# Second norm on GpSimd and ScalarE, output projection in two double banks of PSUM

## Chip, core and metric

The kernel runs on one core of a Trainium2 chip. The metric is the device time of one execution in microseconds. The kernel before took 1049.43 us (median of 3 runs, 1049.25 to 1049.82).

## What is computed

One decoder block on x of 1024 tokens by 1024 features, in float32: RMSNorm, input projection, eight heads of forgetting attention beside a gated spatial mix, output projection with residual, a second RMSNorm, a gated MLP with a causal convolution of width 3, residual, and a final RMSNorm. The part that the change touches is this:

```python
def rmsnorm(x, gain):
    xf = x.astype(jnp.float32)
    y = xf * lax.rsqrt(jnp.mean(xf * xf, axis=-1, keepdims=True) + EPS)
    return y.astype(x.dtype) * gain
...
        mix = jnp.concatenate([att, sg], axis=-1)
        h = h + mix @ w_out[layer]
        h = h + conv_ffn(rmsnorm(h, norm_ffn_g[layer]), w_up[layer], conv_w[layer],
                         conv_b[layer], w_down[layer])
```

## The kernel before

Every float32 product on PE is written as three passes over rounded parts: high by high, high by low, low by high. A "split" makes the two parts: ScalarE (ACT) rounds the value, VectorE (DVE) subtracts the rounded part (`split_w`, L157 to L166). The big products are done in seven instead of eight block products, so sums and differences of blocks of the weights and of the activations are needed as well.

The program is written in the order of the work, and a scheduler that builds each engine's instruction stream decides what stands where. Each engine then works its stream strictly in order. `after(tc, a, b)` (L64) tells the scheduler that a may not stand ahead of b.

Attention (L1138 on) works through eight heads. For each head PE makes the logits of a block of 128 queries in a place of PSUM that is two banks wide (`place()`, two such places, tag "L", four banks), DVE and ACT turn them into weights in SBUF, PE turns these around (`turn_p`, L1026), ACT rounds and DVE subtracts (L1027, L1028), and PE multiplies them with the values (L1042). The turned blocks and the value sums lie in the four other banks (tag "b"). Head 7 has no logits of a next head beside it. After it, the last pair of heads is scaled (`pair_half(3)`, L955 to L958: DVE, ACT, DVE), once the sums of its rows have come back by DMA (L943).

Then comes the stage of the change, the output projection and the second norm (L1196 to L1365). Eight tiles of 128 tokens, in the order 0, 4, 1, 5, 2, 3, 6, 7. Each has two halves of 512 columns, `hf` 0 and 1, and each half takes 12 matmuls of 128x512: four pairs of heads k = 0 to 3 by three passes (`wmm`, L1279 to L1281). k = 3 needs the last pair of heads (the tile G_3837 in the instruction streams).

- At the start of the stage the PSUM pool of attention is given back and a new one with eight single banks is taken (four "b", four "s"). For the first four tiles (0, 4, 1, 5), k = 0 to 2 of all eight halves, 72 matmuls, come before the first matmul with k = 3.
- `hadd` (L1289, DVE) adds a half to the residual that was loaded into `h2`.
- `norm2` (L1296 to L1300): ACT squares the tile from SBUF into the SBUF tile `xn` with a running sum, takes the root; DVE takes the reciprocal and makes `xn` = h2 * r * gain in one instruction of 128x1024 (L1299). `h2` is stored to DRAM.
- `flip` (L1317 on): PE turns `xn` around in two groups of four 128x128 transposes into two "s" banks; ACT and DVE split the result into the operands `XB` of the MLP (B11, B21 from tiles 0 to 3; T2, T3 from tiles 4 to 7).
- Beside this, the first two weight blocks of the MLP are prepared: `upw_a` splits A11 and A12 on ACT and DVE (L166, tiles `wha`), `upw_b(..., inplace=True)` makes four sums of blocks on GpSimd (POOL, L1251 to L1259).

After tile 7, PE starts the MLP's products (`product`, L1372): two with B11 and B21, then the turn of tile 7, two more, then those with T2 and T3. The MLP and the down projection fill the rest of the time.

Of the kernel before, what the change touches and what calls it, by code (L numbers as in the profile page):

```python
# [14 lines left out]
P = 128  # L15
# [54 lines left out]
def block_kernel(ctx: ExitStack, tc: tile.TileContext, xT, xtok, wuv, wv0, wva, wvk, wvl, wqk, cpk, bfv,  # L70
# [1030 lines left out]

    STEPS = [[(h, g) for g in GROUPS[n:n + 2]] for h in range(8) for n in range(0, 9, 2)]
# [99 lines left out]
    psa.release()  # L1202
    psa = tc.alloc_tile_pool(name="psc", bufs=4, space=bass.MemoryType.PSUM, reuse_waits="tile")
# [39 lines left out]
    def upw_b(i, out, inplace=False):  # L1243
# [5 lines left out]
        if inplace:  # L1249
            s = [a21, ut_(upl, "sg", [P, 512], F32, 4), a11, a12]  # L1250
            pool.tensor_tensor(out=a11, in0=a21, in1=a11, op=ALU.add)  # L1251
            pool.tensor_tensor(out=s[1], in0=a11, in1=a22, op=ALU.add)
            pool.tensor_tensor(out=a21, in0=a21, in1=a22, op=ALU.add)
        else:
            s = [ut_(upl, "sg", [P, 512], F32, 4) for _ in range(4)]
            pool.tensor_tensor(out=s[0], in0=a21, in1=a22, op=ALU.add)  # L1256
            pool.tensor_tensor(out=s[1], in0=s[0], in1=a11, op=ALU.add)  # L1257
            pool.tensor_tensor(out=s[2], in0=a21, in1=a11, op=ALU.add)
        pool.tensor_tensor(out=s[3], in0=s[1], in1=a12, op=ALU.add)  # L1259
# [13 lines left out]
    normed = {}  # L1273

    def wmm(tt, hf, ps, ks_):
        ts_ = slice(tt * P, (tt + 1) * P)
        for k in ks_:
            w = wo[k][hf]
            pe.matmul(ps, attT[k][:, 0, ts_], w[:, 0, :], start=(k == 0), stop=False)  # L1279
            pe.matmul(ps, attT[k][:, 0, ts_], w[:, 1, :], start=False, stop=False)  # L1280
            pe.matmul(ps, attT[k][:, 1, ts_], w[:, 0, :], start=False, stop=(k == 3))  # L1281
# [5 lines left out]
    def hadd(tt, hf, ps):  # L1287
        o = slice(hf * 512, hf * 512 + 512)
        x = dve.tensor_tensor(out=h2[tt][:, o], in0=ps, in1=h2[tt][:, o], op=ALU.add)  # L1289
        if tt == 5:  # L1290
            after(tc, x, normed[1])

    def norm2(tt):
        xn[tt] = ut_(xtp, "xn", [P, 1024], F32, 2)
        r = ss2[:, tt:tt + 1]
        act.activation(xn[tt], h2[tt], AF.Square, accum_out=r)  # L1296
        act.activation(r, r, AF.Sqrt, bias=eps[:, 0:1], scale=1.0 / 1024)
        dve.reciprocal(r, r)
        normed[tt] = dve.scalar_tensor_tensor(out=xn[tt], in0=h2[tt], scalar=r, in1=g2b, op0=ALU.mult, op1=ALU.mult)  # L1299
        sp.dma_start(out=h2d[tt], in_=h2[tt])  # L1300
# [8 lines left out]
    def flip(tt):  # L1309
# [3 lines left out]
        for kh in range(2):  # L1313
            ps = sbank()
            for j in range(4):
                k = 4 * kh + j
                pe.transpose(ps[:, j * P:(j + 1) * P], xn[tt][:, k * P:(k + 1) * P], ident)  # L1317
            pp.append(ps.rearrange("p (k t) -> p k t", k=4))
# [17 lines left out]

    WA = [upw_a(i) for i in range(AHEAD)]
    W = [WA[0][1](("A11", "A12"))]
    first = (0, 4, 1, 5)
    banks8 = {(tt, hf): (bank() if hf == 0 else sbank()) for tt in first for hf in range(2)}  # L1340
    for hf in range(2):
        for tt in first:
            wmm(tt, hf, banks8[tt, hf], (0, 1, 2))
# [475 lines left out]
```

## Time and profile before

| | |
|---|---|
| time, median of 3 | 1049.43 us |
| the profiled execution's own time | 1049.38 us |
| span of its trace | 1047.7 us |
| PE busy | 1037.6 us, 99% of the span |
| DVE busy | 891.8 us, 85% |
| ACT busy | 563.4 us, 54% |
| POOL busy | 217.7 us, 21% |
| granted TensorE clock | 0.999 |
| the stage of the change | 360.82 us (first matmul of the projection) to 410.27 us (first product of the MLP) |

Times in the trace are counted from the start of the span. A row of the timeline has start, length, engine, line, operation, output and inputs, the number of instructions that were merged, and in brackets how long the engine had been idle and who released it. PE is the matmul itself and PEld the load of its weights. Matmuls overlap: one of 128x512 is listed with 0.39 us but the next starts some 0.23 us after it. The engine queue of DMA issues is SPq.

### The profile page before, as it was taken

The numbers are of one execution on the slowest core, as the hardware profiler recorded it, in microseconds if no ns is written. First come the engines' busy times: TensorE is split into PE (matmuls) and PEld (weight loads), VectorE is DVE, ScalarE is ACT, GpSimd is POOL, SyncE is SP. The second block draws the span as 40 slices with busy tenths as digits, with TensorE's granted clock in tenths as the row PEclk, the third lists the DMA queues.
The fourth block names the chain that finished last, engine by engine and source line by source line (L and its number), as shares of the span: only waits on it lengthen the run. The fifth ranks groups of instructions, "written<-read, shape, count | busy, mean of one in ns | idle before, by whom it ended". The sixth has DMA issues, their size and how long they took to land.

```text
span 1047.7 us, 14269 instructions
## 1 busy us (share of the span) xinstructions
PE 1037.6 (99%) x4998; PEld 869.5 (83%) x4998; DVE 891.8 (85%) x1302; ACT 563.4 (54%) x1003; POOL 217.7 (21%) x165
## 2 busy tenths in 40 slices
PE   9999999999999999999999999999999999999997
PEld 6988888988888888788888888888888888888886
DVE  6898887888888779998999989898997866897774
ACT  6777632457767747644444444444444544454654
POOL 0000241500422540253333323323331000000000
PEclk9999999999999999999999999999999999999999
DMA  9622558795745533232254431432322998333432
GB/s 326 237 87 86 159 155 245 224 260 174 205 138 171 184 139 141 80 103 79 96 174 162 131 121 60 131 121 70 131 81 81 320 336 297 105 98 101 142 119 101
DMA packets 67451, 161.66 MB, mean 154 GB/s; under 512 B 8094, under 2 KB 9238, under 8 KB 67380
## 3 DMA queue, kind: packets, MB, share of 16 engines
q1 hardware_dynamic: 67108, 160.72, 47.7%
q8 instruction: 39, 0.64, 0.3%
q14 instruction: 32, 0.26, 0.1%
q10 hardware_dynamic: 272, 0.04, 0.0%
HBM read 115.68 MB, written 45.05 MB: 153 GB/s over the span
## 4 chain that ended last, share of the span: by engine, by line
PE 92%; DVE 3%; DMA 2%; ACT 1%; issue 1%; SPq 1%; ACTq 0%; DVEq 0%
PE k L1632 20%; PE qc L1372 11%; PE qa L1372 11%; PE qd L1372 11%; PE qb L1372 5%; PE ps L270 5%; PE pb L270 5%; PE pb L1042 3%; PE pb L1026 2%; PE qc L510 2%; PE qa L510 2%; PE qd L510 2%; PE pl L979 2%; PE pl L978 2%; PE pf L1066 1%; PE pf L1068 1%
## 5 line engine op out<-in xcount | busy, mean ns | idle before, releaser
L1632 PE MATMUL k<-whb,wha 128*128 128x512 f32 (+1 forms) x936 | 209.9, 386 | 0.0
L1632 PEld LDWEIGHTS k<-whb,wha 128*128 128x128 f32 x936 | 174.1, 188 | 35.8 <-DVE wha L166 0.2
L1372 PE MATMUL qc<-xT,whb 128*128 128x512 f32 x540 | 129.9, 389 | 0.1
L1372 PE MATMUL qa<-xB,wha 128*128 128x512 f32 x528 | 127.4, 390 | 0.0
L1372 PEld LDWEIGHTS qc<-xT,whb 128*128 128x128 f32 x540 | 101.3, 188 | 21.6 <-ACT whb L160 0.5
L1372 PEld LDWEIGHTS qa<-xB,wha 128*128 128x128 f32 x528 | 98.8, 188 | 20.8 <-DVE wha L166 0.4
L160 ACT CAST wha<-sg 128x512 fp32r<-128x512 f32 x77 | 47.8, 622 | 96.9 <-PE k L1632 83.9
L160 ACT CAST whb<-sg 128x512 fp32r<-128x512 f32 x82 | 50.6, 618 | 87.3 <-PE qc L1372 67.1
L166 DVE TENSOR_TENSOR wha<-sg,wha 128x512 fp32r<-128x512 f32 x77 | 52.8, 687 | 39.2 <-ACT wha L160 39.1
L1372 PE MATMUL qd<-xB,whb 128*128 128x512 f32 x264 | 63.7, 389 | 0.0
L1372 PE MATMUL qd<-xT,whb 128*128 128x512 f32 x264 | 63.7, 389 | 0.0
L1372 PE MATMUL qb<-xT,whb 128*128 128x512 f32 x252 | 61.0, 389 | 0.0
L166 DVE TENSOR_TENSOR whb<-sg,whb 128x512 fp32r<-128x512 f32 x82 | 57.0, 697 | 4.4 <-ACT whb L160 4.3
L1027 ACT CAST pt<-pb 128x512 fp32r<-128x512 f32 x72 | 40.4, 584 | 37.5 <-PE pb L1026 32.5
L1256 POOL TENSOR_TENSOR sg<-raw 128x512 f32<-128x512 f32 x20 | 30.8, 1541 | 140.3 <-DVE whb L166 78.1
L1372 PEld LDWEIGHTS qd<-xT,whb 128*128 128x128 f32 x264 | 49.5, 188 | 10.5 <-DVE u L1479 0.3
L1372 PEld LDWEIGHTS qd<-xB,whb 128*128 128x128 f32 x264 | 49.6, 188 | 10.3
L1028 DVE TENSOR_TENSOR pt<-pb,pt 128x512 fp32r<-128x512 f32 x72 | 47.4, 687 | 10.7 <-ACT pt L1027 10.4
L1372 PEld LDWEIGHTS qb<-xT,whb 128*128 128x128 f32 x252 | 47.2, 188 | 10.0 <-DVE whb L166 0.3
L1042 PE MATMUL pb<-pt,V 128*128 128x512 f32 (+3 forms) x192 | 49.6, 362 | 0.4 <-DVE pt L1028 0.3
L1259 POOL TENSOR_TENSOR sg<-sg,raw 128x512 f32<-128x512 f32 x20 | 33.3, 1667 | 63.5 <-DVE whb L166 63.5
L1257 POOL TENSOR_TENSOR sg<-sg,raw 128x512 f32<-128x512 f32 x20 | 34.8, 1740 | 47.5 <-issue 44.9
(426 smaller groups left out, 2241.1 us busy)
## 6 DMA issues: line engine op xcount, KB each, us to landing
raw<-wup SPq DMA_DIRECT2D x44, 512.0 KB
sg<-hx SPq DMA_DIRECT2D x77, 256.0 KB
hx<-hs SPq DMA_DIRECT2D x44, 256.0 KB
hx<-ca SPq DMA_DIRECT2D x35, 256.0 KB
xT<-wdn SPq DMA_DIRECT2D x28, 256.0 KB
x<-kd SPq DMA_DIRECT2D x24, 256.0 KB
A<-xtok SPq DMA_DIRECT2D x8, 512.0 KB
raw<-wqk SPq DMA_DIRECT2D x8, 512.0 KB
```

Source lines behind the costliest of these rows:

```text
L160: act.copy(h, src)
L166: return eng.tensor_tensor(out=l, in0=src, in1=f32(h), op=ALU.subtract)
L270: pe.matmul(banks[m], xs(n, xi, k)[:, ms], w[:, wi, :], start=(first and k == 0 and c == 0 and (own or m % 2 == 0)), stop=(k == 3 and c == ...
L510: pe.matmul(ps, w[:, wi, ks], xs(n, xi, k), start=(first and c == 0), stop=(c == 11), skip_group_check=True)
L1027: casts.append(act.copy(pt[:, 0, :], ptr))
L1028: los.append(dve.tensor_tensor(out=pt[:, 1, :], in0=ptr, in1=f32(pt[:, 0, :]), op=ALU.subtract))
L1042: seq(pe.matmul(po[half][:, o:o + w], lhs, pt[:, s, c:c + w], start=(new and s == 0), stop=(s == 1 and (half, k) in ((1, 6), (0, 3))), ski ...
L1256: pool.tensor_tensor(out=s[0], in0=a21, in1=a22, op=ALU.add)
L1257: pool.tensor_tensor(out=s[1], in0=s[0], in1=a11, op=ALU.add)
L1259: pool.tensor_tensor(out=s[3], in0=s[1], in1=a12, op=ALU.add)
L1372: pe.matmul(ps, w[:, wi, ks], xb[:, xi, k, :], start=(first and n == 0), stop=(n == 11), skip_group_check=True)
L1632: pe.matmul((banks[bk + m] if ps is None else ps)[:, o], xh[:, xi, ms], wh[:, wi, o], start=((first and p_ == 0 or new) and n == 0), stop= ...
```

## The change

- **The pool.** Attention's PSUM pool stays until the end of the stage. A tile of the projection takes one of the two wide places (`half_of`): `wide[tt]` is 128x1024, and each half is one of its banks. So two tiles can be open, where it was four. `first` shrinks to (0, 4): 36 matmuls come before k = 3. The turns use the four "b" banks, and `flip` gets a floor: its transposes stand behind the last matmul that was written before it.
- **The norm.** After each `hadd`, POOL multiplies the half by the gain into `xn` (128x512). ACT squares the tile with `wide[tt]`, the place in PSUM, as the target that nobody reads. After DVE's reciprocal, ACT scales `xn` in place by r (Copy, 128x1024). DVE's instruction at L1299 is gone.
- **The sums** of the two early weight blocks on POOL are put into four pairs, each behind the gain of the tile 1, 5, 2 or 3.
- The order in which the turns stand: tile 0 is turned between the halves of tile 1, the others behind the next tile's second half.

```diff
+    def half_of(tt, hf):
+        if tt not in wide:
+            wide[tt] = place()
+        return wide[tt][:, hf * 512:hf * 512 + 512]
...
-    psa.release()
-    psa = tc.alloc_tile_pool(name="psc", bufs=4, space=bass.MemoryType.PSUM, reuse_waits="tile")
...
+            sums_ = ((a11, a21, a11), (s[1], a11, a22), (a21, a21, a22), (a12, s[1], a12))
+            ops = [lambda o=o: pool.tensor_tensor(out=o[0], in0=o[1], in1=o[2], op=ALU.add) for o in sums_]
+            parts.extend((ops[:2], ops[2:]))
...
     def hadd(tt, hf, ps):
         o = slice(hf * 512, hf * 512 + 512)
-        x = dve.tensor_tensor(out=h2[tt][:, o], in0=ps, in1=h2[tt][:, o], op=ALU.add)
-        if tt == 5:
-            after(tc, x, normed[1])
+        dve.tensor_tensor(out=h2[tt][:, o], in0=ps, in1=h2[tt][:, o], op=ALU.add)
+        if hf == 0:
+            xn[tt] = ut_(xtp, "xn", [P, 1024], F32, 2)
+        gained[tt] = pool.tensor_tensor(out=xn[tt][:, o], in0=h2[tt][:, o], in1=g2b[:, o], op=ALU.mult)

     def norm2(tt):
-        xn[tt] = ut_(xtp, "xn", [P, 1024], F32, 2)
         r = ss2[:, tt:tt + 1]
-        act.activation(xn[tt], h2[tt], AF.Square, accum_out=r)
+        act.activation(wide[tt], h2[tt], AF.Square, accum_out=r)
         act.activation(r, r, AF.Sqrt, bias=eps[:, 0:1], scale=1.0 / 1024)
         dve.reciprocal(r, r)
-        normed[tt] = dve.scalar_tensor_tensor(out=xn[tt], in0=h2[tt], scalar=r, in1=g2b, op0=ALU.mult, op1=ALU.mult)
+        act.activation(xn[tt], xn[tt], AF.Copy, scale=r)
         sp.dma_start(out=h2d[tt], in_=h2[tt])
...
-    first = (0, 4, 1, 5)
-    banks8 = {(tt, hf): (bank() if hf == 0 else sbank()) for tt in first for hf in range(2)}
+    first = (0, 4)
...
     for tt in (0, 4, 1, 5, 2, 3, 6, 7):
         hload(tt)
         for hf in range(2):
-            if tt in first:
-                wmm(tt, hf, banks8[tt, hf], (3,))
-                hadd(tt, hf, banks8[tt, hf])
-            else:
-                ps = bank()
-                wmm(tt, hf, ps, range(4))
-                hadd(tt, hf, ps)
+            m = wmm(tt, hf, half_of(tt, hf), (3,) if tt in first else range(4))
+            hadd(tt, hf, half_of(tt, hf))
+            if tt == 1 and hf == 0:
+                flip(0, m)
         norm2(tt)
-        if prev is not None:
-            flip(prev)
+        if prev:
+            flip(prev, m)
         prev = tt
+        if tt in (1, 5, 2, 3):
+            for o in parts.pop(0):
+                after(tc, o(), gained[tt])
     late.release()
...
+    psa.release()
+    psa = tc.alloc_tile_pool(name="psc", bufs=4, space=bass.MemoryType.PSUM, reuse_waits="tile")
```

What the scheduler makes of it is seen in the engines' streams. First PE at the end of head 7. The names are the tiles with their numbers: pb are the single banks, pl the wide places, whl and G the weights of the projection or the pairs of heads, pt the turned attention weights, V the values. Before, the last value products are followed by the projection:

```order
L1042 MATMUL pb_3826<-pt_3787,V_1734 128x256 x2
L1042 MATMUL pb_3826<-pt_3795,V_1733 128x512 x2
L1042 MATMUL pb_3826<-pt_3815,V_1733 128x384 x2
L1042 MATMUL pb_3826<-pt_3815,V_1734 128x128 x2
L1279 MATMUL pb_3876<-whl_3715,A_2849 128x512
L1280 MATMUL pb_3876<-whl_3715,A_2849 128x512
```

In the changed kernel the same place reads so:

```order
L1042 MATMUL pb_3826<-pt_3787,V_1734 128x256 x2
L1042 MATMUL pb_3826<-pt_3795,V_1733 128x512 x2
L1106 MATMUL pl_3872<-whl_3723,A_3281 128x512
L1042 MATMUL pb_3826<-pt_3815,V_1733 128x384
L1107 MATMUL pl_3872<-whl_3723,A_3281 128x512
L1108 MATMUL pl_3872<-whl_3723,A_3281 128x512
L1042 MATMUL pb_3826<-pt_3815,V_1733 128x384
L1042 MATMUL pb_3826<-pt_3815,V_1734 128x128 x2
L1106 MATMUL pl_3872<-G_3731,G_3684 128x512
```

Three matmuls of tile 0 (pl_3872) have moved in among the last value products; three more (k = 0) stand singly among the turns ahead of them, so six of the projection's matmuls now stand inside attention.

Then PE at the first matmuls with k = 3 and behind them. Before, each half has its own bank (pb_3876 and ps_3877 are the halves of tile 0, pb_3878 and ps_3879 those of tile 4), and the row that follows the 24 of them is tile 2 in another bank:

```order
L1279 MATMUL pb_3876<-G_3738,G_3837 128x512
L1280 MATMUL pb_3876<-G_3738,G_3837 128x512
L1281 MATMUL pb_3876<-G_3738,G_3837 128x512
L1279 MATMUL ps_3877<-G_3738,G_3837 128x512
L1280 MATMUL ps_3877<-G_3738,G_3837 128x512
L1281 MATMUL ps_3877<-G_3738,G_3837 128x512
L1279 MATMUL pb_3878<-G_3738,G_3837 128x512
```

In the changed kernel tiles 0 (pl_3872) and 4 (pl_3882) alternate, and tile 1 (pl_3960) follows in the place of tile 0:

```order
L1108 MATMUL pl_3872<-G_3738,G_3837 128x512
L1106 MATMUL pl_3882<-G_3738,G_3837 128x512
L1107 MATMUL pl_3882<-G_3738,G_3837 128x512
L1108 MATMUL pl_3882<-G_3738,G_3837 128x512
L1106 MATMUL pl_3872<-G_3738,G_3837 128x512
L1107 MATMUL pl_3872<-G_3738,G_3837 128x512
L1108 MATMUL pl_3872<-G_3738,G_3837 128x512
L1106 MATMUL pl_3882<-G_3738,G_3837 128x512
L1107 MATMUL pl_3882<-G_3738,G_3837 128x512
L1108 MATMUL pl_3882<-G_3738,G_3837 128x512
L1106 MATMUL pl_3960<-whl_3715,A_2849 128x512
```

The second L1106 on pl_3872 (the second half of tile 0) carries a wait for DVE's addition of the first half, because both halves now belong to one tile of PSUM; so does the second half of every tile. The L1106 on pl_3960 carries a wait for ACT's Square of tile 0, the last user of that place.

Last DVE at the same place, where wha are the first weight blocks of the MLP. This is the changed kernel:

```order
L166 TENSOR_TENSOR wha_3866<-raw_3862,wha_3866 128x512
L166 TENSOR_TENSOR wha_3869<-raw_3862,wha_3869 128x512
L166 TENSOR_TENSOR wha_3910<-raw_3864,wha_3910 128x512
L166 TENSOR_TENSOR wha_3913<-raw_3864,wha_3913 128x512
L1295 TENSOR_TENSOR pt_3922<-pl_3872,pt_3922 128x512
L1295 TENSOR_TENSOR pt_3940<-pl_3882,pt_3940 128x512
L1295 TENSOR_TENSOR pt_3922<-pl_3872,pt_3922 128x512
```

And before, with the same four splits ahead of the first addition:

```order
L166 TENSOR_TENSOR wha_3956<-raw_3868,wha_3956 128x512
L166 TENSOR_TENSOR wha_3959<-raw_3868,wha_3959 128x512
L1289 TENSOR_TENSOR pt_3976<-pb_3876,pt_3976 128x512
L1289 TENSOR_TENSOR pt_3976<-ps_3877,pt_3976 128x512
L1289 TENSOR_TENSOR pt_3992<-pb_3878,pt_3992 128x512
```

The four splits still stand ahead of the first addition; what moved is the additions' order, first halves of tiles 0 and 4 and then the second ones.

More of the change, by code (lines that the diff above doesn't have):

```diff
@@ L1100, in wo_load, with wmm @@
             wo.append(w)
+    def wmm(tt, hf, ps, ks_, order=lambda m: m):
+        ts_, m = slice(tt * P, (tt + 1) * P), None
+        for k in ks_:
+            w = wo[k][hf]
+            order(pe.matmul(ps, attT[k][:, 0, ts_], w[:, 0, :], start=(k == 0), stop=False))
+            order(pe.matmul(ps, attT[k][:, 0, ts_], w[:, 1, :], start=False, stop=False))
+            m = order(pe.matmul(ps, attT[k][:, 1, ts_], w[:, 0, :], start=False, stop=(k == 3)))
+        return m
+    def half_of(tt, hf):
+        if tt not in wide:
+            wide[tt] = place()
+        return wide[tt][:, hf * 512:hf * 512 + 512]
+    EARLY = {}
+    wide, done, gained = {}, set(), {}
     STEPS = [[(h, g) for g in GROUPS[n:n + 2]] for h in range(8) for n in range(0, 9, 2)]
@@ L1258, in upw_b @@
             pool.tensor_tensor(out=s[2], in0=a21, in1=a11, op=ALU.add)
[L1259 removed]
+            pool.tensor_tensor(out=s[3], in0=s[1], in1=a12, op=ALU.add)
         src = {"A22": a22, "S1": s[0], "S2": s[1], "S3": s[2], "S4": s[3]}
@@ L1272, in block_kernel @@
     xn = [None] * 8
[L1273 to L1281, printed above, removed]
     def hload(tt):
@@ L1335, in flip @@
         return d
+    parts = []
     WA = [upw_a(i) for i in range(AHEAD)]
     W = [WA[0][1](("A11", "A12"))]
-    first = (0, 4, 1, 5)
-    banks8 = {(tt, hf): (bank() if hf == 0 else sbank()) for tt in first for hf in range(2)}
+    first = (0, 4)
     for hf in range(2):
         for tt in first:
-            wmm(tt, hf, banks8[tt, hf], (0, 1, 2))
+            wmm(tt, hf, half_of(tt, hf), [k for k in range(3) if (tt, hf, k) not in done])
     W.append(WA[1][1](("A11", "A12")))
```

11 lines of the change are left out of this document (5 added, 6 removed).

## The prediction

> **What bounds the kernel now.** I read the page first, for the engine that is always busy and the chain that ended last.
>
> ```profile
> span 1047.7 us, 14269 instructions
> ...
> PE 1037.6 (99%) x4998; PEld 869.5 (83%) x4998; DVE 891.8 (85%) x1302; ACT 563.4 (54%) x1003; POOL 217.7 (21%) x165
> ...
> PE 92%; DVE 3%; DMA 2%; ACT 1%; issue 1%; SPq 1%; ACTq 0%; DVEq 0%
> ```
>
> PE is busy for 1037.6 of 1047.7 us and carries 92% of the chain. An average doesn't say what the changed stage is worth, so next I read that stage, in stretches of 10 us (each engine's busy time and, in brackets, its instructions).
>
> ```profile
> core 0: us, PE busy (x) PEld busy (x) DVE busy (x) ACT busy (x) POOL busy (x), PEclk, DMA share, GB/s
> 350.00:360.00 10.00, 9.05 (x60) 7.32 (x58) 7.70 (x16) 8.16 (x20) 5.57 (x6) 1.00 0.52 173
> 360.00:370.00 10.00, 9.71 (x45) 8.04 (x45) 6.63 (x10) 5.57 (x10) 1.67 (x1) 1.00 0.69 238
> ...
> 390.00:400.00 10.00, 10.00 (x51) 8.35 (x49) 9.76 (x17) 7.03 (x14) 0.00 (x0) 1.00 0.57 201
> 400.00:410.00 10.00, 10.00 (x54) 8.46 (x52) 9.51 (x17) 6.94 (x16) 0.00 (x0) 1.00 0.46 170
> ```
>
> Two things are to be seen. In the projection PE never stops, although DVE is nearly full too (9.76 and 9.51). And the only stretch with idle PE is the end of attention, 350 to 361. So what the change takes off DVE buys nothing here, and whatever new wait it puts on PE is paid in full. The rest of the time is PE's as well (the chain above), so I carry a delay of this stage to the end one to one.
>
> Third, the waits at the end of attention (total us, times, longest), and PE's timeline at the marks that the sum needs.
>
> ```profile
> PEld pb L1026 <- DVE pt L1028: 1.4, 2, 1.1
> PEld pb L1042 <- DVE pt L1028: 0.7, 2, 0.5
> PEld pb L1042 <- ACT pt L1027: 0.4, 1, 0.4
> ```
>
> ```profile
> 352.48 0.66 PE L1026 MATMUL pb<-ident,H 128*128 128x128 f32 x4 [0.89 <-DVE pt L1028]
> ...
> 360.37 0.61 PE L1042 MATMUL pb<-pt,V 128*128 128x384 f32 x3 [0.28 <-DVE pt L1028]
> 360.82 0.45 PE L1279 MATMUL pb<-whl,A 128*128 128x512 f32 x1
> ...
> 369.07 0.39 PE L1279 MATMUL ps<-whl,A 128*128 128x512 f32 x1
> ...
> 377.23 0.39 PE L1279 MATMUL pb<-G,G 128*128 128x512 f32 x1
> ...
> 377.68 0.39 PE L1281 MATMUL pb<-G,G 128*128 128x512 f32 x1
> ...
> 410.27 0.84 PE L1372 MATMUL qa<-xB,wha 128*128 128x512 f32 x3
> ```
>
> From 369.07 to 377.23 stand 36 matmuls: 0.227 us each. From 360.82 to 410.27 (49.45 us) stand 192 matmuls (43.6) and six turns of eight transposes, so a turn costs 1.0 us. A tile costs PE 24 x 0.227 + 1.0 = 6.4 us.
>
> **The change, part by part.** All in the trace's time, whose execution took 1049.38 us, 0.05 under the median of the runs shown.
>
> *Early matmuls.* Six matmuls (1.36 us) now stand in the end of attention, where the loads waited 2.5 us in all. Four stand directly ahead of a listed wait and cost nothing there (0.91 gained); the two others I count at a third (0.14). Gain 1.05 us, bounds 0 and 1.36.
>
> *Removed from DVE:* eight instructions at L1299, 10.2 us. PE waited for none in the table above, so I count 0.
>
> ```profile
> L1299 DVE SCALAR_TENSOR_TENSOR xn<-pt,ss,g2b 128x1024 f32<-128x1024 f32 x8 | 10.2, 1280 | 0.1
> ```
>
> *First wait: the second half behind the first addition.* The rows of DVE from the last pair of heads to the first addition:
>
> ```profile
> 364.96 1.29 DVE L956 TENSOR_TENSOR H<-H 128x512 f32<-128x512 f32 x2 [2.64 <-DMA H<-rsd]
> 366.34 1.29 DVE L958 TENSOR_TENSOR G<-H,G 128x512 fp32r<-128x512 f32 x2
> 367.55 4.68 DVE L166 TENSOR_TENSOR wha<-raw,wha 128x512 fp32r<-128x512 f32 x4
> 378.11 0.69 DVE L1289 TENSOR_TENSOR pt<-pb,pt 128x512 f32<-128x512 f32 x1 [5.87 <-PE pb L1281]
> ```
>
> Before, PE had 72 matmuls to do until it needed the last pair of heads, and came to it at 377.23, ten microseconds after DVE was through (367.63). Now there are 36. Counted from 360.82 - 1.05 = 359.77, PE reaches k = 3 at 359.77 + 36 x 0.227 = 367.94. That is 0.3 us behind L958, so this cover is all but gone, though not broken. It does the first halves of tiles 0 and 4 (six matmuls) until 369.30. Then the second half of tile 0 needs the addition of its first half. DVE's queue has the four splits at L166 ahead of that. Two in a row take 1.29 us, 0.60 + 0.69, so four end a pitch after 367.55 + 4 x 0.60 = 369.95. (They took 4.68 before, with POOL's sums beside them; the sums now come later.) The addition takes 0.69, and from a matmul's end (377.68 + 0.39) to DVE's start (378.11) pass 0.04: ready at 370.68. **PE waits 1.38 us.** Bounds: 0.7 if DVE starts that addition before the splits, 3.7 if the splits take 4.68.
>
> *Second wait: the place.* Tile 1 takes tile 0's place, which is free when ACT has squared tile 0. The rows of ACT in this stage (count, total, mean ns):
>
> ```profile
> L1296 ACT ACTIVATE xn<-pt 128x1024 f32<-128x1024 f32 x8 | 8.5, 1064 | 14.1 <-DVE pt L1289 14.1
> ...
> L1306 ACT CAST xB<-ps 128x512 fp32r<-128x512 f32 x8 | 4.4, 592 | 3.6 <-PE ps L1317 3.5
> ...
> L1395 ACT CAST xT<-xtB 128x1024 fp32r<-128x1024 f32 x4 | 4.0, 1052 | 0.0
> ...
> L1296 ACT ACTIVATION_READ_ACCUMULATOR xn<-pt 128x1 f32 x8 | 1.5, 191 | 0.0
> ```
>
> The last matmul of tile 0 starts 0.45 after 370.68 and ends at 371.52; the addition ends at 372.25; the Square and its sum take 1.06 + 0.19 with some 0.07 of overlap, until 373.47; PE goes on at 373.51. It had finished tile 4 at 370.68 + 6 x 0.227 = 372.04. **PE waits 1.47 us.** No row shows ACT writing to PSUM. Below, it could take the 0.96 of two casts at L1306 less their overlap; above, 1.25, the sum of the two rows. I take 1.18, nearest to the same instruction into SBUF. The bounds are 0.2 us apart on each side.
>
> *Third: the turn of tile 0* needs POOL's gains and ACT's scaling. POOL takes 1.28 us with DVE idle and 1.62 to 1.74 beside DVE:
>
> ```profile
> 368.32 1.67 POOL L1251 TENSOR_TENSOR raw<-raw,raw 128x512 f32<-128x512 f32 x1 [12.75 <-DVE wha L166]
> ...
> 371.64 1.74 POOL L1253 TENSOR_TENSOR raw<-raw 128x512 f32<-128x512 f32 x1
> ...
> 374.59 1.28 POOL L1251 TENSOR_TENSOR raw<-raw,raw 128x512 f32<-128x512 f32 x1
> ```
>
> Three gains from 370.68 end at 374.5. ACT squares tile 4 until 374.6, two roots and DVE's reciprocal end at some 375.2, and the scaling (1.05, as L1395) at 376.25. PE has done tile 1's first half at 373.51 + 12 x 0.227 = 376.23: no wait worth counting. With POOL at 1.74 it is 0.7.
>
> *Later places.* In the middle, a turn and five or more matmuls (2 us and more) lie between a tile's last matmul and the next use of its place, and the release takes about 0.2 + 0.7 + 1.2 = 2.1. Tile 7 is the exception: after tile 3's second half only a turn and three matmuls of tile 6 (1.7 us) stand ahead of tile 7's first matmul, and ACT's stream has the cast of that turn ahead of the Square, which then ends 0.6 (first four transposes) + 0.6 (cast) + 1.2 = 2.4 us after tile 3. **0.7 us.** Between tile 7's halves nothing stands at all: 0.16 of pipeline, 0.04, 0.69, 0.04 and the DVE queue, **1.0 us** (bounds 0.9 and 1.6, one more DVE instruction). Each of the four stalls restarts PE as at 360.82 (0.45 instead of 0.39): 0.2 us together.
>
> *Moved without cost:* ACT's eight scalings (8.4 us) find 3 us of ACT idle in each 10; the sums of POOL are first needed for the products with T2, some 13 us after tile 7; the loads and stores of `h2` keep their order on SP but for one load that passes a store, ten microseconds before its use. If those covers go, ACT delays the Squares, which is the third wait's mechanism.
>
> Sum: -1.05 + 1.38 + 1.47 + 0.7 + 1.0 + 0.2 = **+3.7 us**; with 0.15 for the small waits at each of the other turns, 3.85. 1049.38 + 3.85 = 1053.2, and 1053.3 against the median.
>
> **Rivals.**
>
> *POOL becomes the bound.* A middle tile has two gains and two sums: 5.1 us at 1.28, 6.7 at 1.67, 7.0 at 1.74, against PE's 6.4. From 1.6 us an instruction POOL falls behind, and ACT's scaling and PE's turn with it. For it speaks what DVE and POOL do to each other (minimum, median and longest ns over the whole run):
>
> ```profile
> L166 DVE TENSOR_TENSOR wha<-raw,wha x44: 676/679/1783, 367.6 to 788.1; 128x512 fp32r<-128x512 f32 x44
> ...
> L1258 POOL TENSOR_TENSOR sg<-raw,raw x20: 1282/1677/2280, 439.1 to 788.3; 128x512 f32<-128x512 f32 x20
> ```
>
> At 1.74 the four tiles in the middle fall behind by (7.0 - 6.4) x 4 = 2.4 us, and the first turn by the 0.7 above: 3.1 more than the forecast, 1056.4. At the longest, 2.28, it is (9.1 - 6.4) x 4 = 10.8 more, near 1064. Against it: the instruction of 1.28 us a tile that DVE loses at L1299 had two tiles of SBUF as inputs, and of what DVE keeps in the middle the additions read one of theirs from PSUM. Nothing in this stage shows POOL beside such additions, so the median near 1.7 keeps its weight.
>
> [...]
>
> *The other side, faster.* If DVE's four splits end before PE asks for the first addition, and the Squares end before PE asks for a place, the idle time of PE in the end of attention is all that counts. All of the 2.5 us of listed waits filled, none of the four handovers over 0.1: -2.5, 1046.9. It decides in its favour only where the handovers together stay under 0.4 us. The rows of the first two alone give 2.85, and the wait between tile 7's halves has nothing at all to cover it.
>
> *About the same.* The handovers cost half of what I count: DVE takes the addition before the splits (0.7 instead of 1.38), the Square costs 0.96 and its wait shrinks with it, and the place of tile 7 is free in time. Then the sum is -1.36 + 0.7 + 1.25 + 0 + 0.9 + 0.2 = +1.7: 1051.1.
>
> *It doesn't do what it says.* The six matmuls stand where PE wasn't idle and save nothing: +1.05, 1054.3. This lies inside the forecast's own range.
>
> **How the numbers follow.** A measurement of this kernel can tell about 0.2%, 2.1 us, from no change. The forecast, handovers as summed with their bounds (+2.1 to +6.5), gets .60; POOL as the bound .19; about the same .16; faster .05. The predicted time is 1053.3. The range goes from 1050.9, inside the third case, to 1058.0, which holds POOL at 1.74 and the upper bound of the first wait (3.7 instead of 1.38: 1055.6) with some of both; it leaves out the faster case, part of the case of about the same, and POOL at its longest. Slower by over 0.2%: .60 + .19 = .79; within: .16; faster: .05.
>
> **What would show it.** In the changed profile's timeline: PE idle before the second L1106 on tile 0's pl, released by DVE's L1295 (1.4 us); before tile 1's first L1106, released by ACT's L1302 (1.5); before tile 7's first L1106 and between its halves (0.7 and 1.0). The waits of attention's end should be about 1 us shorter. The first product of the MLP should start near 414 instead of 410.27, and from there on the two traces should run parallel; if they drift apart later, the one-to-one carrying is wrong. L1298 near 1.28 clears POOL; at 1.6 or more the turns of the middle (L1323) wait for ACT's scaling. L1302 shows what a Square into PSUM costs. I am wrong if PE goes through the stage without these four gaps, if DVE's splits take 4.68 us again, or if something outside the projection moves by more than a microsecond.

## The result, and the profile after

The changed kernel takes **1060.37 us** (median of 4 runs, 1058.12 to 1063.64), against 1049.44 for the kernel before, measured together with it: ratio 1.0106, 95% interval 1.0091 to 1.0122. It is slower by 10.9 us; forecast were 3.9, with 1058.0 as the upper end. Measured again, it took 1058.88 against 1049.42 (ratio 1.0095, 1.0079 to 1.0110).

The page of the profiled execution (1058.12 us, the fastest of the four) shows the shift in three lines:

```profile
span 1056.4 us, 14302 instructions
...
PE 1039.1 (98%) x4998; PEld 869.2 (82%) x4998; DVE 888.3 (84%) x1294; ACT 570.6 (54%) x1011; POOL 237.9 (23%) x181
...
PE 85%; DVE 6%; ACT 4%; DMA 3%; issue 1%; SPq 0%; DVEq 0%; ACTq 0%
```

PE is as busy as before (1039.1 against 1037.6) in a span that is 8.7 us longer, and its part of the chain (the work that ended last, followed back) fell from 92% to 85%. The time is in gaps. Who ended them is told by PE's waits over the whole execution (total us, times, longest):

```profile
PE pl L1106 <- DVE pt L1295: 2.2, 2, 1.4
PE qc L1382 <- DVE u L1493: 2.1, 1, 2.1
PE pl L1106 <- ACT pl L1302: 1.9, 2, 1.3
...
PE qb L1382 <- DVE whb L166: 0.8, 1, 0.8
```

And where they stand, by PE's timeline:

```profile
362.21 0.59 PE L1042 MATMUL pb<-pt,V 128*128 128x384 f32 x3
...
370.65 0.39 PE L1108 MATMUL pl<-G,G 128*128 128x512 f32 x1
372.42 0.50 PE L1106 MATMUL pl<-G,G 128*128 128x512 f32 x1 [1.38 <-DVE pt L1295]
372.75 0.40 PE L1107 MATMUL pl<-G,G 128*128 128x512 f32 x1
...
375.35 0.50 PE L1106 MATMUL pl<-whl,A 128*128 128x512 f32 x1 [1.29 <-ACT pl L1302]
...
405.92 0.50 PE L1106 MATMUL pl<-whl,A 128*128 128x512 f32 x1 [0.60 <-ACT pl L1302]
...
413.40 0.50 PE L1106 MATMUL pl<-whl,A 128*128 128x512 f32 x1 [0.85 <-DVE pt L1295]
...
417.05 5.72 PE L1382 MATMUL qa<-xB,wha 128*128 128x512 f32 x24
...
438.95 0.96 PE L1382 MATMUL qb<-xT,whb 128*128 128x512 f32 x3 [0.78 <-DVE whb L166]
...
473.13 3.02 PE L1382 MATMUL qc<-xT,whb 128*128 128x512 f32 x12 [2.10 <-DVE u L1493]
```

The first four gaps are those of the forecast, in the same places, with the same releasers. Attention's last group of matmuls starts at 362.21 instead of 360.37, 1.84 later. Of this 1.79 us stand there already at 346.59, where a group of turns began at 344.80 before: they were lost in stages whose instructions the change doesn't touch. The MLP's first product starts 6.78 later than before (417.05 against 410.27); without these 1.84, and without one turn of 1.0 us that stood behind that product before and now stands ahead of it, the stage lost 3.9 us. A gap costs more than its listed idle time. At the first one, the matmul behind it starts 1.77 us after the one ahead, where the pitch is 0.227 and the listed idle time 1.38, and the next follows after 0.33: some 0.27 us come on top. The last two gaps, 0.78 and 2.10 us, lie in the MLP, where the forecast had none. 1.84 + 3.9 + 0.78 + 2.10 = 8.6 of the 8.7 us.

So there were four things to settle: whether the four gaps have the causes that the prediction gave, what makes the gap at 473, whether the 1.84 us belong to the change, and why the other runs are up to 5.5 us longer still than the profiled one.

### The profile page after: what moved, and what is told of

It reads as the page before. It is cut to its first block, busy times and chain, and to the rows that moved or that the text cites. A ratio compares the mean times of both kernels' runs of the same rounds, so it can differ in the third digit from the quotient of the medians.

```text
span 1056.4 us, 14302 instructions
## 1 busy us (share of the span) xinstructions
PE 1039.1 (98%) x4998; PEld 869.2 (82%) x4998; DVE 888.3 (84%) x1294; ACT 570.6 (54%) x1011; POOL 237.9 (23%) x181
## 4 chain that ended last, share of the span: by engine, by line
PE 85%; DVE 6%; ACT 4%; DMA 3%; issue 1%; SPq 0%; DVEq 0%; ACTq 0%
PE k L1642 20%; PE qc L1382 10%; PE qd L1382 10%; PE qa L1382 10%; PE qb L1382 5%; PE pb L1042 3%; PE ps L270 3%; PE pb L1026 2%; PE qc L510 2%; PE qd L510 2%; PE qa L510 2%; PE ps L854 2%; PE pb L270 2%; PE pl L979 2%; PE pl L978 2%; PE pf L1066 1%
```

## The experiments

The theory at the outset: the two wide places make the loss, by waits in the projection, and a changed order of DVE in the MLP adds 2.1 us. The rival: the norm's work on POOL and ACT makes it. Each time below is compared with that of the kernel before, measured together with it.

**The changed kernel again.**

> The changed kernel once more, nothing edited. Theory: its loss has three parts that can be seen in the first trace: new gaps of PE in the projection (1.38 + 1.29 + 0.60 + 0.85 us), a gap of 2.1 us in the MLP at 473 us (DVE's L1493 comes late), and 1.8 us that are lost before 107 us, in a stage with the same instructions as before. The first two should be found again within 0.3 us each, and the third should be another size, since it hangs on when loads land. Rival: the 1.8 us are found again within 0.3 us, so they belong to the program. The runs that take 1059 to 1064 us should, by the theory, owe it to the start or the clock, not to the projection.

1058.88 us, 9.5 above before. The gaps came again (1.81, 1.28, 0.60, 0.86, 0.76, 2.06), but attention ended early this time, before even the old kernel, and yet the first product starts at the same place. PE's and DVE's rows of this execution say why, and two rows of DVE in the first trace are there to compare:

```profile
359.98 0.57 PE L1042 MATMUL pb<-pt,V 128*128 128x384 f32 x3
...
368.63 0.47 PE L1106 MATMUL pl<-G,G 128*128 128x512 f32 x1 [1.20 <-ACT G L957]
...
416.86 5.72 PE L1382 MATMUL qa<-xB,wha 128*128 128x512 f32 x24
```

```profile
366.54 1.29 DVE L956 TENSOR_TENSOR H<-H 128x512 f32<-128x512 f32 x2 [4.65 <-DMA H<-rsd]
```

```profile
366.68 1.29 DVE L956 TENSOR_TENSOR H<-H 128x512 f32<-128x512 f32 x2 [2.55 <-DMA H<-rsd]
...
369.27 2.49 DVE L166 TENSOR_TENSOR wha<-raw,wha 128x512 fp32r<-128x512 f32 x4
```

The 1.84 us at the start are not the program's: the same program lost nothing there this time. Over all the traces with two places, the group of turns that is listed at 354.27 in the first one starts anywhere from 351.56 on, and at 352.48 in the kernel before. But what it gained was used up. DVE's L956, which scales the last pair of heads, waits for a load of row sums, and L956 could start only 6.56 us after attention's last group (366.54 - 359.98), in the first trace 4.47, in the kernel before 4.59. Before, PE asked for the result ten microseconds later; now it waits for it: 1.20 us ahead of the pair itself, and 0.43 more than in the first trace at the next gap. This was a new question: what does the load wait for?

**The norm alone.**

```diff
-        xn[tt] = ut_(xtp, "xn", [P, 1024], F32, 2)
-        act.activation(xn[tt], h2[tt], AF.Square, accum_out=r)
+        act.activation(sq, h2[tt], AF.Square, accum_out=r)
...
-        normed[tt] = dve.scalar_tensor_tensor(out=xn[tt], in0=h2[tt], scalar=r, in1=g2b, op0=ALU.mult, op1=ALU.mult)
+        act.activation(xn[tt], xn[tt], AF.Copy, scale=r)
```

> The kernel before (eight banks, four tiles open, old order of the sums) with the new norm alone: POOL multiplies by the gain, ACT scales; ACT's Square goes into a small SBUF tile of 2 KB a partition instead of the two wide places, which this version doesn't have. DVE's order in the MLP is that of before. Theory (the PSUM places make the loss): within 1.5 us of the kernel before, 1048.5 to 1051. Rival (the norm's move to POOL and ACT makes it): 1055 or more.

1050.62 us, ratio 1.0012 (1.0003 to 1.0020). The norm's move costs 1.2 us in the old layout; two turns now wait for ACT's scaling:

```profile
PE ps L1317 <- ACT xn L1299: 1.6, 2, 0.9
```

The rival is out as the cause of the loss in the old layout.

**The places alone**, with the old norm.

```diff
-        gained[tt] = pool.tensor_tensor(out=xn[tt][:, o], in0=h2[tt][:, o], in1=g2b[:, o], op=ALU.mult)
...
-        act.activation(wide[tt], h2[tt], AF.Square, accum_out=r)
+        act.activation(xn[tt], h2[tt], AF.Square, accum_out=r)
...
-        act.activation(xn[tt], xn[tt], AF.Copy, scale=r)
+        dve.scalar_tensor_tensor(out=xn[tt], in0=h2[tt], scalar=r, in1=g2b, op0=ALU.mult, op1=ALU.mult)
```

> The changed kernel with the old norm: ACT squares into SBUF, DVE makes the product in one instruction of 128x1024. The two wide places, the order and the early matmuls stay, and DVE's order in the MLP is that of the changed kernel. Theory: most of the loss stays, 1054 to 1059; the first gap of the projection is still 1.4 us, the place is free 1.2 us earlier (after the addition, no Square into it), and the gap at 473 us stays near 2 us. Rival (the norm's move makes the loss): 1051 or less.

1070.75 us, 21.3 above before: the sign is the theory's, the size is far outside what I expected. PE's waits, a row of DVE at the first of them, and the granted clock (the column after PE's busy time) show three causes:

```profile
PE pl L1106 <- DVE pt L1295: 11.0, 4, 3.9
```

```profile
368.14 4.62 DVE L166 TENSOR_TENSOR wha<-raw,wha 128x512 fp32r<-128x512 f32 x4
```

```profile
388.00:392.00 4.00, 2.38 (x11) 1.00 0.21 26
392.00:396.00 4.00, 3.40 (x8) 0.59 0.27 109
```

The longest wait, 3.94 us, is the first one, and no product of the norm stands ahead of it. There the four splits take 4.62 us, where they take 2.49 in the changed kernel. POOL's sums run beside them, from 368.90 us on: in the changed kernel they stand behind a gain on POOL itself, here only behind an addition on DVE (`gained` in the edit), and that did not hold them back. So this run undoes more than the norm. At the three other waits (2.22, 1.96 and 2.90 us) the product of 1.28 us does stand in DVE's queue ahead of the additions. And behind the gaps the clock falls, to 0.59 in the second stretch above. With the new norm, the same places cost 9.5 us instead of 21.3. How much of these 11.9 us is the product on DVE, how much the sums held back, the target of the Square and the clock, no run here separates.

**DVE's order in the MLP.** Between the two kernels, DVE's stream in the MLP has the same 685 instructions, and four splits of weights among the first 38 stand at other places. Where PE is made to wait it looks like this, before and after the change:

```profile
458.35 1.27 DVE L1422 SCALAR_TENSOR_TENSOR ca<-h,cp,ca 128x1023 f32<-128x1023 f32 x1
459.55 0.68 DVE L1479 TENSOR_TENSOR u<-qb,u 128x512 f32<-128x512 f32 x1
...
463.52 0.67 DVE L1483 TENSOR_TENSOR u<-u,qc 128x512 f32<-128x512 f32 x1
```

```profile
465.17 1.27 DVE L1432 SCALAR_TENSOR_TENSOR ca<-h,cp,ca 128x1023 f32<-128x1023 f32 x1
466.36 1.78 DVE L166 TENSOR_TENSOR whb<-sg,whb 128x512 fp32r<-128x512 f32 x1
468.07 0.68 DVE L1489 TENSOR_TENSOR u<-qb,u 128x512 f32<-128x512 f32 x1
...
472.40 0.68 DVE L1493 TENSOR_TENSOR u<-u,qc 128x512 f32<-128x512 f32 x1
```

A split of 1.78 us now stands ahead of a result that PE needs: L1493 ends 8.9 us later than its counterpart L1483, while PE at this place is only some 6 us later. The experiment adds order constraints that put the stream back to what it was:

```diff
+        if i == 1:
+            for s_, x in (((2, "S2"), ("m", 0)), ((2, "A12"), ("d", 1)), ((2, "A22"), ("conv", NFF + 1)),
...
+                after(tc, M[s_], M[x])
+        if i == 2:
+            for s_, x in ((("conv", 1), ("u2", 2)), ((3, "S2"), ("conv", 1)), (("m", 1), (3, "S2")), ((3, "S3"), ("u3", 2))):
+                after(tc, M[s_], M[x])
```

> The changed kernel, with DVE's order in the first steps of the MLP put back to that of before by twelve order constraints (no wait on another engine). Theory: the gap of 2.1 us at 473 us comes from the order alone, so it vanishes and the time is 1.5 to 2.5 us below the changed kernel in the same call. Rival: DVE comes late out of the projection, whatever its order; then a gap of 1.5 us or more stays before the same product and the time is within 0.7 us of the changed kernel.

1055.06 us, 3.8 below the changed kernel, measured together with it. The gap is gone; the product that waited now follows the one ahead of it at its pitch:

```profile
469.22 2.88 PE L1384 MATMUL qd<-xT,whb 128*128 128x512 f32 x12
471.94 2.88 PE L1384 MATMUL qc<-xT,whb 128*128 128x512 f32 x12
```

So the order alone made the gap. From the product with qb to the end of the span, this trace takes 615.2 us and the first one of the changed kernel 617.4, both with the clock at 1.00 around this place: 2.2 us, the gap. The median fell by 1.6 us more. The clock, shown next, can do that, but no kept trace of the changed kernel has it falling here.

**Square into SBUF.**

```diff
-        act.activation(wide[tt], h2[tt], AF.Square, accum_out=r)
+        act.activation(sq, h2[tt], AF.Square, accum_out=r)
```

> The changed kernel with one edit: ACT squares into a small SBUF tile (bf16, 2 KB a partition) instead of into the wide place, so the place is free after the second addition. Theory: the gaps before tile 1 (1.29 us) and before tile 7 (0.60 us), released by ACT's Square, fall to 0.3 us or less together, and those released by DVE's additions (1.4 to 1.8 and 0.85 us) stay: 1.0 to 1.9 us below the changed kernel (1058.9), near 1057.4. Rival: the place waits for DVE's additions anyway, so the gap only changes its releaser and the time stays within 0.5 us of the changed kernel.

1055.69 us, 6.8 above before (the changed kernel: 9.5). Both gaps that ACT's Square ended are gone, those that DVE's additions ended stay (2.7 us). A Square takes 1.06 us into SBUF and 1.03 into PSUM: its price was never at issue, only that the place waits for it.

This trace also shows what a gap can cost beside its own length. The product behind the gap of 2.1 us, here at 469.62, and in the timeline of the changed kernel above at 473.13:

```profile
469.62 4.60 PE L1383 MATMUL qc<-xT,whb 128*128 128x512 f32 x12 [2.08 <-DVE u L1494]
```

```profile
468.00:472.00 4.00, 2.38 (x6) 0.71 0.35 131
472.00:476.00 4.00, 4.00 (x17) 0.86 0.40 131
```

The same twelve matmuls after the same gap take 4.60 us here and 3.02 there; here the granted clock fell to 0.71 and 0.86 in the two stretches, there it stayed at 1.00. Seven traces of this study have this gap: in three (the places alone, this one, and halves apart) the twelve matmuls take 4.48 to 4.60 us, in four 3.02. A gap of two microseconds thus costs 2.1 in one execution and 3.7 in another. Shorter gaps can do it too: in the run with DVE's old order, gaps of 1.12 and 1.82 us close together left the clock at 0.58 over 372 to 376 us, while 1.20 and 1.81 at the same place in the changed kernel's second trace left it at 1.00. The spread of the changed kernel fits this: of its eight runs, the three above 1061 us have a mean granted clock of 0.995, the five others 0.998 or 0.999, and 0.0035 of 1060 us is an estimated 3.7 us. Where in those three runs the clock fell isn't shown, since none of them is a kept trace. Why one and the same gap has two outcomes isn't shown either.

**Halves in banks of their own**, turns in the wide places, Square into SBUF.

```diff
-        if tt not in wide:
-            wide[tt] = place()
-        return wide[tt][:, hf * 512:hf * 512 + 512]
+        if (tt, hf) not in wide:
+            wide[tt, hf] = bank()
+        return wide[tt, hf]
...
-            ps = bank() if floor is not None else sbank()
+            ps = pl2[:, kh * 512:kh * 512 + 512] if floor is not None else sbank()
```

> As the run with Square into SBUF, and the two kinds of banks change their roles: each half of a tile has a bank of its own (tag b), the turns take the wide places. So no half waits for the addition of its own tile's first half. Six instead of twelve banks' worth of claims stay two tiles deep as before. Theory: all four gaps of the projection (4.1 us in the first trace) shrink to 0.8 us or less together, some of the early matmuls are lost (only three now stand before attention's last matmul, 0.7 us), and the gap of 2.1 us in the MLP stays: 1054 to 1056. Rival: two tiles of depth are too few whatever the grain of the waits; gaps of 2 us or more stay and the time is 1056.5 or more.

1058.24 us, the rival's time, but not for the rival's reason. All four gaps of the projection are gone. The two behind ACT's Square went with its move into SBUF, as in the run before; the two behind DVE's additions went with the banks, although DVE's L956 started 4.52 us after attention's last group, as late as in the first trace. So these two need the shared place. Other waits stand in PE's list:

```profile
PE qa L1384 <- DVE t L1339: 3.0, 1, 3.0
PE qc L1384 <- DVE u L1495: 2.1, 1, 2.1
PE pl L1324 <- ACT xn L1305: 1.2, 2, 0.6
```

The MLP's first product takes the banks in which the last turn lay, and waits 3.0 us until DVE has read them. I hadn't thought of who takes the banks next.

**The splits behind the first additions.**

```diff
+        if tt == 4 and hf == 0:
+            for s_ in early_splits:
+                after(tc, s_, x)
```

> The changed kernel with DVE's four early splits of the weights (wha) behind the first additions of tiles 0 and 4 instead of ahead of them. Theory: the first gap (1.4 to 1.8 us, second half of tile 0) falls by 1.2 us or more, to at most 0.5 us, and since the wait for the place of tile 0 follows it in a chain, that one stays near 1.3 us: 0.9 to 1.5 us below the changed kernel. Rival: the four splits only change places, and the second additions, which now stand behind them, cost the same at the place of tile 1: no change within 0.5 us.

1061.94 us, 13.1 above before, worse than the changed kernel; the theory fell. DVE's rows:

```profile
371.60 4.24 DVE L166 TENSOR_TENSOR wha<-raw,wha 128x512 fp32r<-128x512 f32 x4
375.76 1.28 DVE L1298 TENSOR_TENSOR pt<-pl,pt 128x512 f32<-128x512 f32 x2
```

The four splits took 2.49 us where POOL was idle; now they run beside POOL's first gains and take 4.24, with the second additions behind them. The place of tile 0 comes free late, and PE waits 4.97 us instead of 1.29. The splits ahead of the additions, where the change leaves them, are at the better of the two places.

**The cures at once**, with the late splits and the turns' banks among them.

> All the cures at once on the changed kernel: a bank for each half, Square into SBUF, the splits behind the first additions, DVE's order in the MLP as before; the norm stays on POOL and ACT. Theory: no gap over 0.5 us is left in the projection or the MLP, so the time is that of the kernel before plus what POOL's gains and ACT's scalings make the turns wait (1.2 us in the run with the norm alone), less up to 0.7 us of early matmuls: 1049 to 1051. Rival: something of the two-deep order still costs, for instance the last pair of heads, whose cover is 36 instead of 72 matmuls; then PE waits 1 us or more for L958 or L957 and the time is 1051.5 or more.

1056.90 us, 8.1 above before: the theory missed, because two of its cures were none. The splits took 5.75 us beside POOL, a reciprocal stood behind them, and a turn waited 3.22 us; and the first product waited 3.03 us for the turns' banks, as in the run with halves apart:

```profile
377.88 1.09 PE L1332 MATMUL pl<-ident,xn 128*128 128x128 f32 x8 [3.22 <-ACT xn L1313]
```

**The row sums' load first.** In SP's stream two weight loads of 512 KB, and one load of `h2`, stood ahead of it; here they follow.

```diff
+        after(tc, d, tails[7])
+        for x in wloads if tt == 1 else ():
+            after(tc, x, d)
...
-    sp.dma_start(out=g2b, in_=g2r.to_broadcast((P, 1024)))
+    after(tc, sp.dma_start(out=g2b, in_=g2r.to_broadcast((P, 1024))), tails[7])
```

> The changed kernel with one edit on SP: the load of the last pair's row sums (H from rsd, L943) is issued ahead of the second pair of weight loads and of the loads of h2 and of the gain; these follow it. In the traces so far that load landed 3.1 to 6.3 us after attention's last matmul began (4.1 before the change). Theory: it lands some 2 us earlier, DVE's L956 with it, so the first gap (1.4 to 1.8 us, and up to 1.2 us before the last pair itself) falls by 1 to 2 us in all: 1056.5 to 1058.2. Rival: the load takes its time from the round trip of the stored sums and not from the other loads; DVE's L956 begins no more than 0.5 us earlier after attention's last matmul and the time stays within 0.7 us of the changed kernel (1058.9).

1056.40 us, 7.1 above before, where the changed kernel has 9.5. PE's and DVE's rows:

```profile
361.75 0.57 PE L1044 MATMUL pb<-pt,V 128*128 128x384 f32 x3
```

```profile
364.68 1.29 DVE L958 TENSOR_TENSOR H<-H 128x512 f32<-128x512 f32 x2 [1.01 <-DMA H<-rsd]
```

The pair is ready to be scaled 2.93 us after the start of attention's last group, instead of 4.4 to 6.6 in the traces without this edit, and the first gap is gone altogether, although the two halves still share a place. So it was mainly the other loads, and not the round trip, that this load waited for. And the first gap takes two things at once, a shared place and a late DVE.

**Both additions behind both halves**, with Square into SBUF and DVE's old order in the MLP.

```diff
             m = wmm(tt, hf, half_of(tt, hf), (3,) if tt in first else range(4))
-            hadd(tt, hf, half_of(tt, hf))
             if tt == 1 and hf == 0:
                 flip(0, m)
+        for hf in range(2):
+            hadd(tt, hf, half_of(tt, hf))
```

> Wide places and six early matmuls as changed; Square into SBUF, DVE's MLP order as before the change, and both halves of a tile are multiplied before the first of its two additions is written, so that the second half has no addition to wait for. Theory: no gap between halves any more; at the places of tile 1 and tile 7 at most 1 us together; no gap in the MLP over 0.8 us: 1050 to 1052. Rival: the waits only move to the places, since a place is now free two additions after its last matmul; gaps of 2 us or more in the projection and 1052.5 or more.

1051.04 us, ratio 1.0015 (1.0006 to 1.0023). Written in this order, no half has an addition to wait for. What is left in PE's waits from 356 us on:

```profile
PE qb L1386 <- DVE whb L166: 1.1, 1, 1.1
PE pl L1106 <- DVE pt L1297: 1.1, 1, 1.1
PE pl L1106 <- ACT G L957: 0.6, 1, 0.6
PE pb L1325 <- ACT xn L1307: 0.5, 2, 0.3
```

**The same, with the row sums' load first.**

> The run with both additions last, with the row sums' load first as well. Theory: the early matmuls' gain (1.2 us) is kept and at most 1 us of gaps is left in the projection: 1048 to 1050.5, the same as the kernel before. Rival: PE still waits for the splits, the additions or the turns of the first two tiles by 2 us or more: 1051 or more.

1049.34 us against 1049.26, ratio 1.0002 (0.9993 to 1.0011): the changed kernel with four cures is as fast as the kernel before, and no faster. From 356 us on only two kinds of waits are left:

```profile
PE qb L1394 <- DVE whb L166: 1.1, 1, 1.1
PE pb L1333 <- ACT xn L1315: 0.6, 2, 0.3
```

Together they are 1.7 us, about what the early matmuls brought (1.3). No version here beats the kernel before.

**Halves apart, with the MLP's first products in the other banks** and DVE's old order.

```diff
+    psq("c")
+
     ahead = []
```

> Halves in banks of their own, turns in the wide places, Square into SBUF, DVE's MLP order as before, and the MLP's first products in the banks of the halves instead of those of the turns (in the run without this, the first product waited 3.0 us for DVE's reads of the last turn). The four splits stay ahead of the additions. Theory: the gap of 3.0 us and that of 2.1 us are gone, the turns wait 1.2 us for ACT's scaling: 1050 to 1052. Rival: the first product's wait moves to the additions of the last tile and stays at 1.5 us or more: 1052.5 or more.

1051.36 us, ratio 1.0017 (1.0008 to 1.0026). The 3.0 us at the first product are gone: that gap was the banks'. Left are 1.4 us in turns that wait for ACT's scaling, and 0.9 at the product with qb.

The losses, each as the step between two kernels of the table (us above the kernel before, measured together with it):

| kernel | above before |
|---|---|
| changed, again | 9.5 |
| with DVE's old order in the MLP | 5.6 |
| with Square into SBUF | 6.8 |
| with the row sums' load first | 7.1 |
| old order, Square into SBUF, additions last | 1.8 |
| the same, load first | 0.1 |

One by one the first three cures bring 3.8, 2.6 and 2.3 us, and the load first brings 1.7 on top of the others. The additions last were not run alone: 9.5 - 3.8 - 2.6 - 1.8 = 1.3 is what is left for them if the first two simply add up. Together the four cures take away the whole loss.

## Why the prediction was wrong

**Right: the early matmuls.** Forecast a gain of 1.05 us. The waits of PE's loads at attention's end fell from 2.5 to 1.4 us, with six matmuls more in almost the same time: of their 1.36 us, 0.05 show (1.84 against 1.79), a gain of 1.3.

**Right: the four handovers.** Forecast 1.38, 1.47, 0.7 and 1.0; measured 1.38, 1.29, 0.60 and 0.85, each with the releaser that was named. The runs with halves apart and with additions last show that the first and the last need the tile that both halves share, and the run with Square into SBUF that the two others come from the Square. The splits took 2.49 us (forecast 2.4) with POOL's sums out of the way, and 4.62 in the run in which the sums came early. But that the first wait agrees to the hundredth is luck: it was 1.81 us in the second trace, and nothing with the load first.

The stage as a whole was forecast at +3.7 to 3.85 and measured at +3.9 in the first trace, and that agreement is luck as well. The early matmuls brought 0.25 more than forecast and the four idle times were 0.4 shorter (4.1 against 4.55), but what PE loses around the gaps beside the idle time was counted at 0.2 us and came to 1.1 (four times 0.27).

**Right: DVE's instruction at L1299 counts 0** in the old layout (the norm alone is no gain). In the new layout it need not be: in the run with the places alone it stands ahead of the additions for which PE waits 2.22, 1.96 and 2.90 us. What it is worth there by itself isn't shown, since that run differs in more than this instruction.

**Right: POOL doesn't become the bound.** L1298 takes 1350 ns in the mean, below the point of 1.6. Two of its gains show what stood beside them. That of 1.31 us runs beside DVE's L1337, which has one of its inputs in PSUM. That of 1.74 starts while DVE's L1309 is at work, whose two inputs lie in SBUF, and takes longer; DVE's L1342, which starts behind that gain, again with two inputs in SBUF, takes 1.78 us, where its counterpart L1334 took 0.69 and 0.68 us before the change, with POOL idle:

```profile
383.02 1.31 POOL L1298 TENSOR_TENSOR xn<-pt,g2b 128x512 f32<-128x512 f32 x1 [2.35 <-DVE pt L1295]
...
387.24 1.74 POOL L1298 TENSOR_TENSOR xn<-pt,g2b 128x512 f32<-128x512 f32 x1
```

```profile
382.86 0.68 DVE L1337 TENSOR_TENSOR xtB<-xtB,pb 128x512 f32<-128x512 f32 x1
...
386.65 1.18 DVE L1309 TENSOR_TENSOR xT<-t,xT 128x512 fp32r<-128x512 f32 x1
387.76 1.78 DVE L1342 TENSOR_TENSOR xtB<-t,xtB 128x512 f32<-128x512 f32 x1
```

That the place of the inputs makes the difference is a reading of these rows; no run tests it. The prediction kept POOL's median near 1.7 because nothing in the stage showed POOL beside DVE's additions. The trace before the change does show it: a sum of 1.29 us beside two additions of 0.69 us, each with one input in PSUM.

```profile
378.45 1.29 POOL L1259 TENSOR_TENSOR raw<-sg,raw 128x512 f32<-128x512 f32 x1
```

```profile
378.79 0.69 DVE L1289 TENSOR_TENSOR pt<-ps,pt 128x512 f32<-128x512 f32 x1
379.47 0.69 DVE L1289 TENSOR_TENSOR pt<-pb,pt 128x512 f32<-128x512 f32 x1
```

**Wrong: "I carry a delay of this stage to the end one to one."** This is the step that failed, and the largest part of the miss. In the MLP DVE is nearly full as well (20.00 of 20 us from 440 to 460 before the change), so there PE hangs on the order of DVE's queue. I compared the orders of the projection and never those behind it. The scheduler had moved four splits there. With the order put back, the gap of 2.1 us was gone and the median 3.8 us lower; 2.2 of these the traces show as the gap, the rest is argued. The prediction itself named the sign of it ("if they drift apart later"), without a price or a chance.

**Wrong in size: the cover of the last pair of heads.** "That is 0.3 us behind L958, so this cover is all but gone" took L958's end from one execution, in which the load of row sums came 4.6 us after the start of attention's last group. Over the traces it came 4.4 to 6.6 us after it. While ten microseconds of cover lay over it, no time of the kernel before could show this. With the cover at 0.3, the second trace shows 1.20 us of wait for the pair and 0.43 more at the next gap, and the runs with the load first put 1.7 to 2.3 us on it.

**Missing: what a gap does to the clock.** I counted 0.05 us for each restart of PE; the trace has some 0.27 for each gap. And a gap of 2 us can be followed by about 1.6 us of lost clock (4.60 against 3.02 for twelve matmuls). The mean granted clocks of the runs from 1058 to 1063.6 us fit this; the forecast's upper end had no term for it.

**What stays open.** Why the first trace lost 1.84 us before attention: the same program lost nothing there the next time, so it is no part of the change, but its cause wasn't tried. What makes PE wait for DVE's split at the product with qb (0.5 to 1.1 us in most versions with two places, none in the kernel before): it is there with DVE's old order too (0.77), and wasn't tried. And at which gap the clock falls: 1.38 and 1.29 us close together left it at 1.00 in the changed kernel's first trace, 1.12 and 1.82 brought it to 0.58 with DVE's old order; a gap of 3.03 left it at 1.00 with the halves apart and brought it to 0.57 in the cures at once, and the gap of 2.1 us in the MLP lowered it in three of the seven traces that have it.

## What to carry to other kernels

When cover over a wait is taken away (72 matmuls to 36), the spread of what it covered becomes part of the time: look up in several executions how late that can come, and what stands ahead of it in the DMA queue. Compare each nearly full engine's order to the end of the program, not only in the stage that was edited. And write a buffer's producers ahead of its first reader: if two halves share a tile, the order in which they are written decides whether one waits for a reader of the other.

## What the runs showed of the hardware that I had not expected

- After a gap of 2.1 us in PE the granted clock fell in three traces out of seven, to 0.61 at the lowest over a stretch of 4 us; the same twelve matmuls took up to 4.60 us in them and 3.02 in the others.
- Gaps of 1.12 and 1.82 us close together were followed by a granted clock of 0.58 over 4 us in one trace; 1.20 and 1.81 at the same place left it at 1.00 in another.
- Four splits on DVE take 2.49 us with POOL idle, 4.62 beside POOL's sums (4.68 before the change) and 4.24 to 5.75 us beside POOL's gains.
- A load of 256 KB that was wanted at once let DVE start 2.9 us after the start of attention's last group with the other loads behind it, and 4.4 to 6.6 us with three of 512 KB ahead of it.
